# A hybrid decoder block on one core: the branch gates ahead of the branches, 24 of them in pairs by seven block products

## Chip, cores and metric

One core of one Trainium2 chip. The metric is the device time of one execution in microseconds (us).

## What is computed

One layer on 512 tokens of width 2048, in float32: an adaLN-modulated norm, one input projection whose columns go to a gated linear recurrence (HGRN2, 8 heads), to a sliding-window attention and to two sets of branch gates, then a squared-ReLU MLP.

```python
ada = c_act @ w_ada + b_ada                      # six vectors of 2048
h = modulate(rms_norm(x, g1), shift1, scale1)    # (512, 2048)
proj = h @ w_in                                  # hq hf hi hg | aq ak av | gate_hg gate_at
o_hg = rms_norm(hgrn2_chunkwise(...)) * silu(hg)
o_at = sink_swa(q, k, v, sinks, table)
merged = sigmoid(gate_hg) * (o_hg @ w_branch_hg) + sigmoid(gate_at) * (o_at @ w_branch_attn)
x = x + gate1 * (merged @ w_out)
h2 = modulate(rms_norm(x, g2), shift2, scale2)
x = x + gate2 * (square(relu(h2 @ w_ff1)) @ w_ff2)
```

## The kernel before

Everything is held transposed: channels on the 128 partitions, the 512 tokens along the free axis. A product of float32 matrices is made of three matmuls (`mm3`): both operands are split into a high part (a copy by ScalarE) and a low part (a subtraction by VectorE), and high x high, high x low and low x high are added up in PSUM. An output tile of 128 channels over 2048 inputs is 16 x 3 = 48 matmuls of 512 columns.

The work of TensorE is a list of items (`add_tile`, `add_item`); one item is a quarter of such a tile (four input tiles, 12 matmuls) with 512 weight columns. `step` runs item after item: it issues the weight loads on SP (`pump_loads`, three buffers `raw`), the splits of the weights up to two items ahead (`pump_splits`, four buffers `wt`), the item's matmuls, its `post` (what reads PSUM), and one entry of the list `todo`. Everything else, attention, recurrent heads, splits of activations, is a generator that a planner (`Plan`) runs from `drive`, twice in an item: it keeps a clock for each of TensorE, VectorE and ScalarE from fixed costs, and takes a generator's next piece, lowest rank first, when its due time has come and the clocks of VectorE and ScalarE are less than 2.5 us ahead of TensorE's (1 us for rank 9). A piece that yields nothing is due again 0.6 us after the end of its work. The planner decides only the order in which instructions are issued to each engine; the chip then runs each engine's list in that order, with semaphores between them. SBUF slots are counted by tag (`take`, `drop`, `room`: `T` 6, `O` 25, `C` 16, `L` 5).

Stages: a start that makes the first adaLN columns and h; 32 tiles of the input projection for attention and the recurrent heads; then the branches; `wout`; the MLP. In the branch stage (loop at lines 596 to 605) gate tiles and branch tiles alternate: a gate tile (48 matmuls over h) leaves its sigmoid in a slot `T` (`gate_post`), and the branch tile that follows one (first branch) or three (second) gate tiles later (`SKEW`) multiplies its 24 matmuls' result by it (`branch_post`). The last unit of `attention` splits its output at once; that of the recurrent heads is split by `split_hg` after the last tile of the first branch. `ada_rest` (line 397, rank 9) makes the other four adaLN vectors meanwhile: 256 steps, each a load of 256 KB by SP into one of three buffers and a multiply-and-sum by VectorE with a broadcast row `aa` that is loaded once in 16 steps.

```python
while state["item"] < n_start + PACE * n or 0 < len(mg) < KT:
    yield "wait"
```

In the MLP, pairs of output tiles are made with seven block products (Strassen's scheme in Winograd's form) in place of eight: tokens in two halves of 256, inputs and outputs in pairs of tiles (`seven_pair`, line 895). A pair is four units; each is one item of 2 x 7 x 3 matmuls of 256 columns, with seven sums and differences of weight blocks: three are loaded, two more are loaded into a slot `S` to which GpSimd's accumulating DMA adds a fourth block (`pump_loads`), and two are added by VectorE (`split_seven`); a unit takes two of the four `wt` buffers. The input's combinations (`t_sums`, `t_split`) are made once. `sums1` to `sums3` join the seven results, from banks that are four `mx` or one `mx` and three `acc`.

Of the kernel before, what the change touches and what calls it, by code (L numbers as in the profile page):

```python
# [17 lines left out]
P = 128  # L18
# [9 lines left out]
PACE = 1.35  # L28
# [5 lines left out]
SKEW = (1, 3)  # L34
# [57 lines left out]
def tile_block(ctx, tc, xT, cT, wada1, wada2, badaT, g1T, g2T, wg0, win, wbat, wbhg, wout, wfg, wfp, wst,  # L92
               wff2, lbT, hggT, qgT, kgT, sinks, table, ident_d, mask_d, onehot_d, neg_d, outT):
# [243 lines left out]
    def pump_loads():  # L337
        done = items[state["split"]][0] if state["split"] < len(items) else len(loads)
        while state["load"] < len(loads) and state["load"] < done + BUFS["raw"]:
            src, n = loads[state["load"]]  # L340
            if state["load"] in doubled and not room("S") and not room("T", 5):
                return
            raw = act.tile([P, n], F32, tag="raw", bufs=BUFS["raw"], name=nm("raw"))
            if state["load"] in doubled:
                n -= 2 * P
                raw = raw[:, 0:n]
                full, src = src, src[:, 0:n]
            SP.dma_start(out=raw, in_=src)
            if state["load"] in doubled:
                c = 2 * P  # L350
                tag = "S" if room("S") else "T"
# [45 lines left out]
    def ada_rest():  # L397
# [11 lines left out]
        for g in range(4):  # L409
            for q in range(4):  # L410
# [5 lines left out]
                for i in range(16):  # L416
                    fetch(n)
                    while state["item"] < n_start + PACE * n or 0 < len(mg) < KT:
# [6 lines left out]
                    yield  # L425
# [116 lines left out]

    def gate_post(br, n):
        def post(ps):
# [3 lines left out]
            sig[br, n] = t  # L548
        return post

    def branch_post(br, n):
        def post(ps):
# [8 lines left out]
            drop("T")  # L561
            if (br, n) == (0, KT - 1):
# [28 lines left out]
    def gates_done(ps):  # L591
        gate_post(1, KT - 1)(ps)
        drop("A", 32)
        pl.spawn(split_m(), 0)

    for br, wb in ((0, wbat), (1, wbhg)):
        for n in range(KT + SKEW[br]):
            if n < KT:
                add_tile(next_win(), hx, gates_done if (br, n) == (1, KT - 1) else gate_post(br, n))
            if n >= SKEW[br]:  # L600
                def post(ps, br=br, n=n - SKEW[br]):
                    branch_post(br, n)(ps)
                    if br == 1:
                        msdone[n] = True
                add_tile([wb[n - SKEW[br]]], ready(xb[br]), post)

# [39 lines left out]
    HALF = [slice(0, T // 2), slice(T // 2, T)]  # L646
# [3 lines left out]

    def part(xs, c):
        return xs[0][:, c], xs[1][:, c]
# [224 lines left out]
    B22, B11, B12, S1, S3, S2, S4 = range(0, WT, 2 * P)  # L877

    def split_seven(raw, s13, tag):
        hi, lo = wt(), wt()  # L880
        s24 = take("T")
        drop("T")
        c = 2 * P
        sact(hi[:, 0:3 * c], raw[:, 0:3 * c], AF.Copy)
        tt(s24[:, 0:c], s13[:, 0:c], raw[:, c:2 * c], ALU.add)
        tt(s24[:, c:2 * c], s24[:, 0:c], raw[:, 2 * c:3 * c], ALU.add)
        sact(hi[:, 3 * c:5 * c], s13, AF.Copy)
        sact(hi[:, 5 * c:7 * c], s24, AF.Copy)
        tt(lo[:, 0:3 * c], raw[:, 0:3 * c], hi[:, 0:3 * c].bitcast(F32), ALU.subtract)
        tt(lo[:, 3 * c:5 * c], s13, hi[:, 3 * c:5 * c].bitcast(F32), ALU.subtract)  # L890
        tt(lo[:, 5 * c:7 * c], s24, hi[:, 5 * c:7 * c].bitcast(F32), ALU.subtract)
        drop(tag)
        return hi, lo

    def seven_pair(p, now):

        g = p // 2
        cell = {}

        def take_banks():  # L900
            if now:
                cell["b"] = [mx() for _ in range(4)]
            else:
                cell["b"] = [mx()] + [acc() for _ in range(3)]

        def unit(u):
            def emit(hi, lo):
                a, b = HALF
                if u == 0:
                    take_banks()  # L910
                b0, b1, b2, b3 = cell["b"]
                for kp in range(2):
                    j = 2 * u + kp
                    pl.until(lambda: len(tb.get(j, ())) == 4 and isinstance(tb[j][0], tuple))
                    e, o = h2[2 * j], h2[2 * j + 1]
                    t1, t2, t3, t4 = tb[j]
                    first, last = j == 0, j == KT // 2 - 1
                    for ps, c, w, x in ((b0, a, B11, part(e, a)), (b1, a, B12, part(o, a)), (b1, b, S2, t2),
                                        (b2, a, S3, t3), (b2, b, S1, t1), (b3, a, B22, t4), (b3, b, S4, part(o, b))):
                        w += kp * P  # L920
                        mm3(ps[:, c], hi[:, w:w + P], lo[:, w:w + P], x, first and c is a,
                            last and (c is b or ps is b0))
            return emit

        def sums1():
            b0, b1, _, _ = cell["b"]
            e1 = cell["e1"] = take("T", [P, 2, T // 2])
            e2 = cell["e2"] = take("T", [P, 2, T // 2])
            sact(e2[:, 0, :], b0[:, HALF[0]], AF.Copy)
            tt(e1, b1.rearrange("p (n c) -> p n c", n=2), e2[:, 0:1, :].to_broadcast([P, 2, T // 2]), ALU.add)  # L930

        def sums2():
            e1, e2, b2 = cell["e1"], cell["e2"], cell["b"][2].rearrange("p (n c) -> p n c", n=2)
            tt(e2, e1[:, 1:2, :].to_broadcast([P, 2, T // 2]), b2, ALU.subtract)
            tt(e1[:, 1, :], e2[:, 0, :], b2[:, 1, :], ALU.subtract)

        def sums3():
            a, b = HALF
            e1, e2, b3 = cell["e1"], cell["e2"], cell["b"][3].rearrange("p (n c) -> p n c", n=2)
            tt(e2, e2, b3, ALU.add)  # L940
            drop("mx", 4 if now else 1)
# [8 lines left out]
            if now:  # L950
                todo.extend([lambda: hidden(r0, g), lambda: hidden(r1, g)])
# [3 lines left out]
        def post():  # L955
            todo.extend([sums1, sums2, sums3])

        for u in range(4):
            ahead_of[len(items)] = 1 if u < 3 else 2
            ld = add_load(wst[p - 3, u], 1024)  # L960
            doubled.add(ld)
            add_item(ld, 0, 1024, unit(u), None, post if u == 3 else None, split_seven)
# [202 lines left out]
    oat = []  # L1165
# [124 lines left out]
    def attention(c):  # L1290
# [50 lines left out]
        if c == 1:  # L1341
            yield from split_raw(oat, xb[0])
# [175 lines left out]

    ctx.enter_context(tc.manual_schedule())
# [109 lines left out]
```

## Time and profile before

| | |
|---|---|
| median of 3 runs | 2730.06 us (2728.93 to 2730.11) |
| the profiled execution | 2728.55 us, span 2726.8 us |
| TensorE busy | 2698.7 us (99%) |
| TensorE's weight loads | 2289.5 us (84%) |
| VectorE busy | 1683.3 us (62%) |
| ScalarE busy | 1037.1 us (38%) |
| moved by DMA | 415.49 MB, mean 152 GB/s |

PE is TensorE's matmuls and PEld its weight loads, DVE is VectorE, ACT ScalarE, POOL GpSimd and SP the engine whose queue issues most DMAs. L126 and the like are lines of helpers that issue all instructions of a kind (L163 matmuls, L126 sums of two tensors, L159 ScalarE's operations), so groups are told apart by their tiles. Busy shares are averages over stages.

### The profile page before, as it was taken

Reading aid. Unit: us, or ns where it says so; the run is one execution under the profiler, and the core shown is the slowest. Engines: PE = TensorE matmul, PEld = TensorE weight load, DVE = VectorE, ACT = ScalarE, POOL = GpSimd, SP = SyncE. Lnnn points to the kernel's source line nnn. Section 1 sums busy time; section 2 is a strip of 40 time slices with the busy share of each in tenths; the row PEclk is TensorE's granted clock in tenths of the full one; section 3 lists DMA queues with packets and bytes.
Section 4 is the critical chain, followed back from the end, with each engine's and each line's share of the span. In section 5 each row is a group of like instructions: output and inputs, shape, how many; then the busy total and the mean of one; then the engine's idle time right before and its main releaser. Section 6 shows DMA issues by size and latency. Waiting matters only on the chain.

```text
span 2726.8 us, 38611 instructions
## 1 busy us (share of the span) xinstructions
PE 2698.7 (99%) x14718; PEld 2289.5 (84%) x14718; DVE 1683.3 (62%) x3231; ACT 1037.1 (38%) x1913; POOL 153.3 (6%) x144
## 2 busy tenths in 40 slices
PE   8999999999999999999999999999999999999999
PEld 4777777888888888888888899988999988999887
DVE  5778787655444545565467666666566655666664
ACT  4245455544222322232353434333343333434332
POOL 1000000000000000000000101110011100111100
PEclk9999999999999999999999999999999999999999
DMA  8852322344555555556334455654455544555544
GB/s 329 293 182 97 128 89 74 127 137 147 192 182 184 195 187 179 192 168 211 108 93 123 130 134 138 156 141 127 129 144 147 148 129 126 138 147 148 137 126 132
DMA packets 182073, 415.49 MB, mean 152 GB/s; under 512 B 18880, under 2 KB 48704, under 8 KB 181888
## 3 DMA queue, kind: packets, MB, share of 16 engines
q1 hardware_dynamic: 149184, 380.18, 42.4%
q0 software_dynamic: 32704, 32.85, 7.8%
q8 instruction: 116, 1.90, 0.3%
q14 instruction: 69, 0.57, 0.1%
HBM read 408.72 MB, written 4.23 MB: 151 GB/s over the span
## 4 chain that ended last, share of the span: by engine, by line
PE 95%; DVE 3%; ACT 1%; DMA 1%; issue 0%; SPq 0%; POOLq 0%; ACTq 0%
PE acc L163 69%; PE mx L163 25%; PE mx L167 1%; DVE wt L126 1%; DVE T L126 0%; DMA C<-xT 0%; DMA S<-wst 0%; ACT T L159 0%; DVE C L130 0%; DVE L L130 0%; ACT wt L159 0%; DVE B L130 0%; ACT A L159 0%; DVE T L130 0%; DVE s L1242 0%
## 5 line engine op out<-in xcount | busy, mean ns | idle before, releaser
L163 PE MATMUL acc<-A,wt 128*128 128x512 f32 (+1 forms) x5136 | 1134.1, 369 | 4.1 <-ACT A L159 1.9
L163 PEld LDWEIGHTS acc<-A,wt 128*128 128x128 f32 x5136 | 908.7, 189 | 174.9 <-issue 8.6
L126 DVE TENSOR_TENSOR wt<-raw,wt 128x512 fp32r<-128x512 f32 (+1 forms) x828 | 595.8, 724 | 422.7 <-ACT wt L159 419.6
L159 ACT ACTIVATE wt<-raw 128x512 fp32r<-128x512 f32 (+1 forms) x828 | 529.9, 657 | 841.1 <-PE acc L163 592.5
L163 PE MATMUL acc<-B,wt 128*128 128x512 f32 (+1 forms) x3528 | 732.6, 359 | 2.6 <-DVE wt L126 1.2
L163 PEld LDWEIGHTS acc<-B,wt 128*128 128x128 f32 x3528 | 610.1, 189 | 101.8 <-DVE wt L126 1.8
L163 PE MATMUL mx<-A,wt 128*128 128x256 f32 (+1 forms) x2448 | 426.1, 310 | 5.4 <-DVE wt L126 3.0
L163 PEld LDWEIGHTS mx<-A,wt 128*128 128x128 f32 x2448 | 360.6, 192 | 37.0 <-issue 5.0
L163 PE MATMUL mx<-B,wt 128*128 128x256 f32 (+1 forms) x1632 | 297.5, 319 | 0.4 <-DVE wt L126 0.4
L130 DVE SCALAR_TENSOR_TENSOR C<-acc,adaT,C 128x512 f32<-128x512 f32 x210 | 157.3, 749 | 199.5 <-PE acc L163 199.5
L163 PEld LDWEIGHTS mx<-B,wt 128*128 128x128 f32 x1632 | 249.7, 191 | 21.6 <-DVE wt L126 0.9
L354 POOL DMA_DIRECT2D S<-wst x88 | 105.2, 1196 | 2123.0 <-DVE T L126 1203.1
L421 DVE SCALAR_TENSOR_TENSOR ada<-ada,aa 128x512 f32<-128x512 f32 x256 | 175.3, 685 | 45.8 <-DMA ada<-wada 41.2
L163 PE MATMUL acc<-O,wt 128*128 128x512 f32 x768 | 178.6, 389 | 0.0
L163 PEld LDWEIGHTS acc<-O,wt 128*128 128x128 f32 x768 | 144.2, 188 | 29.9
L159 ACT ACTIVATE T<-T 128x256 f32<-128x256 f32 (+1 forms) x218 | 104.4, 507 | 110.2 <-DVE T L126 107.7
L159 ACT ACTIVATE wt<-T 128x512 fp32r<-128x512 f32 x144 | 87.2, 621 | 83.9 <-DVE T L126 79.0
L126 DVE TENSOR_TENSOR wt<-T,wt 128x512 fp32r<-128x512 f32 x144 | 96.2, 684 | 0.0
L126 DVE TENSOR_TENSOR T<-T,raw 128x256 f32<-128x256 f32 x144 | 61.1, 425 | 32.9 <-DMA T<-wst 29.0
L159 ACT ACTIVATE T<-acc 128x512 f32<-128x512 f32 x34 | 20.3, 598 | 160.2 <-PE acc L163 160.2
L159 ACT ACTIVATE B<-T 128x512 fp32r<-128x512 f32 x80 | 47.2, 602 | 47.4 <-DVE T L126 33.1
L126 DVE TENSOR_TENSOR T<-S,raw 128x256 f32<-128x256 f32 x88 | 37.1, 421 | 41.6 <-DMA S<-wst 37.1
(170 smaller groups left out, 1349.9 us busy)
## 6 DMA issues: line engine op xcount, KB each, us to landing
raw<-win SPq DMA_DIRECT2D x128, 512.0 KB, 4.0
ada<-wada SPq DMA_DIRECT2D x256, 256.0 KB, 4.3
raw<-wff SPq DMA_DIRECT2D x128, 512.0 KB, 3.6
raw<-wst SPq DMA_DIRECT2D x116, 384.0 KB, 3.8
O<-wada SPq DMA_DIRECT2D x128, 256.0 KB, 5.1
S<-wst SPq DMA_DIRECT2D x88, 256.0 KB, 3.7
S<-wst POOLq DMA_DIRECT2D x88, 256.0 KB, 4.3
raw<-wout SPq DMA_DIRECT2D x32, 512.0 KB, 4.0
```

Of the source, the lines that this page charges most:

```text
L126: nc.vector.tensor_tensor(out=out, in0=in0, in1=in1, op=op)
L130: nc.vector.scalar_tensor_tensor(out=out, in0=in0, scalar=scalar, in1=in1, op0=op0, op1=op1)
L159: nc.scalar.activation(out=out, in_=in_, func=func, **kw)
L163: PE.matmul(out, lhsT=lhsT, rhs=rhs, start=start, stop=stop)
L167: PE.transpose(out=out, in_=in_, identity=ident)
L354: G.dma_start(out=s.rearrange("p (n c) -> p n c", c=c), in_=full[:, None, 3 * c:4 * c].to_broadcast([P, 2, c]), accum_op=ALU.add)
L421: nc.vector.scalar_tensor_tensor(out=t, in0=t, scalar=1.0, in1=cb, op0=ALU.mult, op1=ALU.mult, accum_out=adaq[:, i, q:q + 1])
```

## The change

The 32 gate tiles come before both branches: first the 16 of attention (branch 0), then the 16 of the recurrent heads (branch 1). The first 8 stay plain tiles; the other 24 are made in 12 pairs by seven block products, with the MLP's code, which moves up into `add_seven` and gets one more call of the planner in a unit. The combinations of h that these need are made by a new generator, `h_blocks` (rank 5), once attention is over, in slots `O` (9), `L` (3) and `C` (15, after the last recurrent head); the last of the four overwrites half of a tile of h. The weight tensor of the 24 tiles is laid out in blocks on the host's side like that of the MLP. The doubled weight loads use slots `L` before the MLP. Sigmoids are written to DRAM by SP (`spill`, taken from `todo` in a later place) and read back ahead of each branch tile, up to three at a time (`sig_load`). Attention's output is split after the last gate pair. The number of items that weights are split ahead is worked out from the `wt` buffers that they hold. `ada_rest` is paced by one step an item, no longer pauses while `merged` is split, and yields `go`, which makes it due again at once.

```diff
-PACE = 1.35
+PACE = 1.0
-SKEW = (1, 3)
+NCG = 8
...
+            slot = "S" if "mlp" in pools else "L"
-            if state["load"] in doubled and not room("S") and not room("T", 5):
+            if state["load"] in doubled and not room(slot) and not room("T", 5):
...
-                    while state["item"] < n_start + PACE * n or 0 < len(mg) < KT:
+                    while state["item"] < n_start + PACE * n:
                         yield "wait"
...
-                    yield
+                    yield "go"
...
             t = take("T")
             sact(t, ps, AF.Sigmoid)
-            sig[br, n] = t
+
+            def spill():
+                SP.dma_start(out=sigd[br, n], in_=t)
+                drop("T")
+            todo.append(spill)
...
+    def sig_load(k):
+        def pre():
+            for i in range(k, min(k + 3, 2 * KT)):
+                if i not in fetched and (i == k or room("T", 2)):
+                    fetched.add(i)
+                    t = sig[i // KT, i % KT] = take("T")
+                    SP.dma_start(out=t, in_=sigd[i // KT, i % KT])
+        return pre
...
+    def h_blocks():
+        a, b = HALF
+        while len(att_done) < 2:
+            yield "wait"
+        homes = ["O"] * 9 + ["L"] * 3 + ["C"] * 15
+        for j in range(KT // 2):
+            own = j < 3
+            tags = [homes.pop(0) for _ in range(4 if own else 3)]
+            while "C" in tags and len(ohg) < NH:
+                yield "wait"
...
+            yield from need("T", 4)
+            e, o = full(h[2 * j]), full(h[2 * j + 1])
+            x, y = take("T"), take("T")
+            tt(x[:, a], e[:, b], e[:, a], ALU.subtract)
+            tt(x[:, b], x[:, a], o[:, b], ALU.subtract)
+            tt(y[:, a], e[:, b], o[:, b], ALU.subtract)
+            tt(y[:, b], o[:, b], o[:, a], ALU.subtract)
+            tt(y[:, b], y[:, b], x[:, a], ALU.subtract)
...
+            split(y, hi, lo)
+            t2 = two(tags[2])
+            split(x[:, b], *t2)
...
+        for j in range(3, KT // 2):
+            while state["item"] < last_plain + j // 2 + 2:
+                yield "wait"
+            e = full(h[2 * j])
+            tt(e[:, a], e[:, b], e[:, a], ALU.subtract)
+            hb[j][0] = part(h[2 * j], b)
+            split(e[:, a], *hb[j][0])
...
+        def post():
+            todo.extend([sums1, sums2, sums3])
+            if done:
+                done()
...
+            sact(e1[:, 0, :], e1[:, 0, :], AF.Sigmoid)
+            sact(e2[:, 0, :], e2[:, 0, :], AF.Sigmoid, scale=-1.0)
+            sact(e1[:, 1, :], e1[:, 1, :], AF.Sigmoid, scale=-1.0)
+            sact(e2[:, 1, :], e2[:, 1, :], AF.Sigmoid)
...
+    def gates_done():
         drop("A", 32)
-        pl.spawn(split_m(), 0)
+        drop("O", 9)
+        drop("L", 3)
+        drop("C", 15)
+        pl.spawn(split_raw(oat, xb[0]), 0)
+        pl.spawn(split_m(), 1)
...
+    for k in range(NCG):
+        last_plain = len(items)
+        add_tile(next_win(), hx, gate_post(k // KT, k % KT))
+    for k in range(NCG, 2 * KT, 2):
+        add_seven([wgt[(k - NCG) // 2, u] for u in range(4)], gate_blocks, k % 4 == 0, gate_joined(k),
+                  gates_done if k == 2 * KT - 2 else None)
...
     for br, wb in ((0, wbat), (1, wbhg)):
-        for n in range(KT + SKEW[br]):
...
+        for n in range(KT):
+            add_tile([wb[n]], ready(xb[br]), branch_post(br, n), sig_load(KT * br + n))
...
+    held_by = [2 if e[6] is split_seven else 1 for e in items]
+    for i in range(len(items)):
+        n = AHEAD
+        while sum(held_by[i:i + n + 1]) > BUFS["wt"]:
+            n -= 1
+        ahead_of.setdefault(i, n)
...
+    pl.spawn(h_blocks(), 5)
     pl.spawn(ada_rest(), 9)
     while state["item"] < len(items):
-        if state["item"] == n_mix:
-            pl.until(lambda: len(oat) == 8)
+        if state["item"] == n_mix + 4 * NCG:
+            pl.until(lambda: len(att_done) == 2)
         step()
```

## Rows read from the trace of the kernel before

**Rows 1.** The page: engine table (busy, share, instructions), and chain that ended last.
```profile
PE 2698.7 (99%) x14718; PEld 2289.5 (84%) x14718; DVE 1683.3 (62%) x3231; ACT 1037.1 (38%) x1913; POOL 153.3 (6%) x144
...
PE 95%; DVE 3%; ACT 1%; DMA 1%; issue 0%; SPq 0%; POOLq 0%; ACTq 0%
```

**Rows 2.** Waits of PE, whole span: us in total, times, longest us.
```profile
PE mx L163 <- DVE wt L126: 3.4, 5, 1.2
...
PE mx L167 <- DVE T L126: 0.9, 2, 0.4
```

**Rows 3.** Timeline of PE, 590 to 706 us: start, length, operation, count.
```profile
592.79 0.33 PE L163 MATMUL mx<-T,C 128*128 128x64 f32 x2
...
643.98 0.33 PE L163 MATMUL mx<-T,C 128*128 128x64 f32 x2
...
684.27 5.60 PE L163 MATMUL acc<-O,wt 128*128 128x512 f32 x24
689.71 11.04 PE L163 MATMUL acc<-A,wt 128*128 128x512 f32 x48
700.59 5.60 PE L163 MATMUL acc<-O,wt 128*128 128x512 f32 x24
```

**Rows 4.** Timeline of PE in a pair of the MLP.
```profile
2007.23 0.52 PE L163 MATMUL acc<-A,wt 128*128 128x256 f32 x3
2007.59 0.52 PE L163 MATMUL mx<-A,wt 128*128 128x256 f32 x3
```

**Rows 5.** Windows: stretch, length, busy us of PE, PEld, DVE, ACT, POOL; PEclk, DMA share, GB/s.
```profile
20.00:60.00 40.00, 36.60 (x166) 22.79 (x161) 22.24 (x46) 15.19 (x27) 0.51 (x1) 0.96 0.91 348
480.00:560.00 80.00, 79.55 (x412) 64.44 (x410) 50.61 (x107) 39.00 (x68) 0.00 (x0) 1.00 0.42 138
560.00:640.00 80.00, 80.00 (x393) 65.28 (x390) 46.31 (x99) 43.55 (x78) 0.00 (x0) 1.00 0.39 125
760.00:960.00 200.00, 200.00 (x884) 165.69 (x883) 100.88 (x225) 55.73 (x95) 0.00 (x0) 1.00 0.57 188
1994.00:2014.00 20.00, 20.00 (x169) 20.00 (x168) 14.39 (x25) 8.21 (x15) 4.79 (x4) 1.00 0.78 187
```

**Rows 6.** Timeline of DVE in a pair of the MLP; brackets: idle before, releaser.
```profile
1999.03 0.42 DVE L126 TENSOR_TENSOR T<-S,raw 128x256 f32<-128x256 f32 x1 [0.88 <-DMA S<-wst]
1999.49 0.43 DVE L126 TENSOR_TENSOR T<-T,raw 128x256 f32<-128x256 f32 x1
...
2006.08 0.96 DVE L126 TENSOR_TENSOR wt<-raw,wt 128x768 fp32r<-128x768 f32 x1 [1.75 <-ACT wt L159]
2006.95 0.68 DVE L126 TENSOR_TENSOR wt<-S,wt 128x512 fp32r<-128x512 f32 x1
2007.55 0.68 DVE L126 TENSOR_TENSOR wt<-T,wt 128x512 fp32r<-128x512 f32 x1
```

**Rows 7.** The page: DMA issues, count, KB each, median us to landing.
```profile
S<-wst SPq DMA_DIRECT2D x88, 256.0 KB, 3.7
S<-wst POOLq DMA_DIRECT2D x88, 256.0 KB, 4.3
```

**Rows 8.** Timeline of DVE, 640 to 940 us.
```profile
648.52 0.69 DVE L421 SCALAR_TENSOR_TENSOR ada<-ada,aa 128x512 f32<-128x512 f32 x1 [1.86 <-DMA ada<-wada]
...
674.90 0.75 DVE L130 SCALAR_TENSOR_TENSOR O<-mx,hgg_sb,C 128x512 f32<-128x512 f32 x1
...
935.86 0.69 DVE L126 TENSOR_TENSOR O<-O,O 128x512 fp32r<-128x512 f32 x1 [4.62 <-ACT O L159]
936.47 0.68 DVE L126 TENSOR_TENSOR wt<-raw,wt 128x512 fp32r<-128x512 f32 x1
```

**Rows 9.** Windows of line 421 alone (steps of ada, two instructions each).
```profile
200.00:480.00 280.00, 17.29 (x50) 1.00 0.28 95
```

**Rows 10.** Tile ada, 480 to 660 us: who waited for it; landing.
```profile
  DVE ada L421: 9.1, 6
...
DMA to landing us min/median/max: 4.0/4.5/5.2
```

More of the change, by code (lines that the diff above doesn't have):

```diff
@@ L541, in tile_block @@
     mg = []
+    sigd = {(br, n): dram.tile([P, T], F32, name=f"sig{br}_{n}") for br in range(2) for n in range(KT)}
     def gate_post(br, n):
@@ new lines, in tile_block, with part, full, two @@
+    hb = {}
+    hbdone = set()
+    att_done = []
+    def part(xs, c):
+        return xs[0][:, c], xs[1][:, c]
+    def full(xs):
+        t = take("T")
+        tt(t, xs[0].bitcast(F32), xs[1].bitcast(F32), ALU.add)
+        return t
+    def two(tag):
+        z = take(tag, [P, 2, T // 2], F32R)
+        return z[:, 0, :], z[:, 1, :]
+    def h_blocks():
[8 more added lines that the diff above has]
+                yield "wait"
+            for tag in set(tags):
+                yield from need(tag, tags.count(tag))
+            yield from need("T", 4)
[6 more added lines that the diff above has]
+            tt(y[:, b], y[:, b], x[:, a], ALU.subtract)
+            drop("T", 2)
+            yield
+            hi, lo = take(tags[0], dt=F32R), take(tags[1], dt=F32R)
+            split(y, hi, lo)
+            t2 = two(tags[2])
+            split(x[:, b], *t2)
+            t1 = None
+            if own:
+                t1 = two(tags[3])
+                split(x[:, a], *t1)
+            drop("T", 2)
+            hb[j] = [t1, t2, (hi[:, a], lo[:, a]), (hi[:, b], lo[:, b])]
+            if own:
+                hbdone.add(j)
+            yield
+        for j in range(3, KT // 2):
+            while state["item"] < last_plain + j // 2 + 2:
+                yield "wait"
+            yield from need("T")
+            e = full(h[2 * j])
+            tt(e[:, a], e[:, b], e[:, a], ALU.subtract)
+            hb[j][0] = part(h[2 * j], b)
+            split(e[:, a], *hb[j][0])
+            drop("T")
+            hbdone.add(j)
+            yield
@@ L875, in ff2_post @@
         return post
[L877 to L893, printed above, removed]
@@ L895, in seven_pair @@
-    def seven_pair(p, now):
[L897 to L937, printed above, removed]
@@ L938, in sums3, with hidden_blocks, joined @@
+    def hidden_blocks(j):
+        a, b = HALF
+        pl.until(lambda: len(tb.get(j, ())) == 4 and isinstance(tb[j][0], tuple))
+        e, o = h2[2 * j], h2[2 * j + 1]
+        return [part(e, a), part(o, a), part(o, b)] + tb[j]
+    def seven_pair(p, now):
+        def joined(e1, e2):
             a, b = HALF
[L939 to L941 removed]
             r0, r1 = take("T"), take("T")
@@ L950, in sums3 @@
             if now:
-                todo.extend([lambda: hidden(r0, g), lambda: hidden(r1, g)])
+                todo.extend([lambda: hidden(r0, p // 2), lambda: hidden(r1, p // 2)])
             else:
                 waiting.extend([r0, r1])
[L955 to L962, printed above, removed]
+        add_seven([wst[p - 3, u] for u in range(4)], hidden_blocks, now, joined)
     def ff2_group(g):
@@ L1340, in attention @@
         drop("O", 4 + 6)
-        if c == 1:
-            yield from split_raw(oat, xb[0])
+        att_done.append(c)
     ohg = []
@@ L1579 @@
              .reshape(8, G0 // 4, P, 1024))
-    win = kxn(w_in[:, sum(tiles[G0:], [])])
+    win = kxn(w_in[:, sum(tiles[G0:NCG - 2 * KT], [])])
+    wgt = sevens(w_in[:, sum(tiles[NCG - 2 * KT:], [])])
     rows = []
```

114 lines of the change are left out of this document (93 added, 21 removed).

## The prediction

> **What bounds the kernel now.** I read the page's engine table and chain first: TensorE is busy 99% of the span and nearly all of the chain that ended last is its matmuls [rows 1]. The list of what TensorE waited for then shows how little it stands: its largest wait on weight splits is 3.4 us in the whole span [rows 2]. So a change pays by the matmul columns that it removes, and loses by each microsecond in which it makes TensorE wait. The profiled execution took 2728.55 us (span 2726.8), 1.5 us under the median of 2730.06; I work against it and add the 1.5 at the end.
>
> **The products saved.** A gate tile is 48 matmuls of 512 columns. In the gate stage one tile takes 700.59 - 689.71 = 10.88 us, 226.7 ns for each [rows 3], so two tiles take 21.76 us. A pair by seven products is 8 x 7 x 3 = 168 matmuls of 256 columns. The MLP already does this: a block of three follows the next at 0.36 us, 120 ns each [rows 4], and not 113.3, since the weight loads there fill the whole window, 20.00 of 20.00 us [rows 5]. A pair is 20.16 us, 1.60 less. Twelve pairs: -19.2 us. The other eight gates and all branch tiles keep their matmuls. The Trainium skill, TensorE: Matmul & The Clock Gate, section Back-to-back issue gap, has N/2.4 + 2.5 ns for a matmul; by it two tiles would take 20.7 us, a pair 18.3, and the saving would be 28 us as an estimate. The rows stand against it at both widths, 226.7 and 120 ns, so it gets no chance as a rival, and the sum keeps the rows.
>
> All that follows is what the change pays for it. The granted clock is 1.00 in every stage concerned [rows 5], and no stall below is long, so I cost nothing for it.
>
> **VectorE's split work in the pairs.** A unit (four to a pair, 5.04 us of TensorE) costs VectorE two sums at 0.46, a split of 768 at 0.87 and two of 512 at 0.60: 3.0 us [rows 6]. The joins of a pair are three operations of 512 and one of 256, 2.3 us, so 0.6 for each unit, and one step of the ada matrix, of the same shape as the splits of 512, is 0.6. Together 4.2 of 5.04 us, 83%, against 50% in the gate stage of before [rows 5]. It fits on average. The MLP runs the same units with 72% of VectorE [rows 5] and TensorE doesn't wait there. The order is the risk: a unit's split can start only when the unit before last has returned its weight buffers, so it has 5.04 us, and the join, which waits for the pair's last products, stands ahead of it on VectorE.
>
> **The doubled loads.** Each unit needs a load (3.7 us) and behind it the accumulating load of GpSimd (4.3) [rows 7], with only two slots (in `L`, as three of its five now hold blocks of h) and a third in `T` once in a pair. The third unit's slot is returned 2.4 us into a unit, and its data are wanted 7.7 us later, while the two loads need 8 and their issues 0.6: about 1 us late. The MLP lives with this lateness: VectorE waits for S there 0.88 us [rows 6], and it is hidden. New is the company: ada steps (256 KB a unit) and spills (128 KB a unit). In the MLP's units the DMA engines are 0.78 busy at 187 GB/s; the gate stage needs 0.57 for 188 GB/s [rows 5]. At that price ada's 52 GB/s adds 0.16, and spills of 26 GB/s some 0.08 to 0.10: 1.02 to 1.04. In the startup 0.91 of busy carried 348 GB/s [rows 5], so a busy engine moves more bytes than these shares say, and I take 265 GB/s to be carried with loads 1 to 2 us later than now. The third unit's split then ends at most about 0.5 us after TensorE wants it. Bounds: 0 (hidden as in the MLP) to 1.2 us a pair, 0 to 14 us; I take 0.2 a pair, 2 us.
>
> **Blocks of h.** `h_blocks` needs for each of 8 pairs of h tiles about 4.3 us of VectorE (two sums of 512, five of 256, splits of 512 and 256), and later 5 times 1.5. Three pairs can be made once attention is over; five need the slots of the last recurrent head, whose last operation is at 674.90 [rows 8]. The gate stage begins near 659 (684.27 less two tiles and 3.6 us of that head [rows 3]); eight plain tiles last 87 us, so the first seven-product unit starts near 750. Between 675 and 750 TensorE runs 27 items, and VectorE has 2.1 us free in each: 57 us for these 21.5 and 7.5 and for ada's 27 steps (16). No wait; bounds 0 to 4, taken 0.5.
>
> **The spills.** SP waits for the sigmoid of each plain gate before it issues the write, behind which stand the next weight load and ada loads. A plain item's weights are split up to three items (8 us) early, and the write is held about 3.3 us: hidden at one ada step an item; 0 to 6 us, taken 1. In the pairs the spill comes one step after the sigmoids and holds nothing.
>
> **The pace of ada.** The step of VectorE that builds the late adaLN columns is asked for once an item (was 1.35), its pause is dropped, and it yields `go`: the planner may put several in a row, as long as its clock for VectorE is under 1 us ahead. Before, at most one went in at a time. By 480 us only 25 steps had run (each shows two instructions) [rows 9]; heads come every 51.2 us [rows 3] with 16 items, so 480 us is item 120 and the new rule wants 72. Some 40 are owed when VectorE gets free. The planner doesn't know what a load costs: three buffers and 4.5 us to landing [rows 10] give three steps in about 5 us, 1.67 us a step, where the plan counts 0.68. VectorE executes in order, so a step whose load is late holds the splits and the recurrence behind it. This is seen already: 1.86 us at 648.52 [rows 8], 9.1 us in six waits over the stage [rows 10], of which TensorE felt little: it waited for such a result twice, 0.4 us at most [rows 2]. With two steps an item, the loads need 3.3 us where an item with its share of the head lasts 3.2. So I expect small delays in bursts of 16 steps (then a pause of two items for the next `aa`), about 1 us in each of five bursts. Bounds 0 to 18; taken 4, and 0.5 more for attention (0 to 4). The steps themselves hide in idle time of VectorE, 58 to 63% busy here [rows 5].
>
> **The two joints.** Before, gate tiles stood between the branches: `split_hg` ran from 935.86 [rows 8] under gates of the second branch. Now branch 1 follows branch 0 at once. VectorE must first multiply the last tile (0.6, after TensorE's end), then make the first low half (0.6): TensorE stands 1.1 us or more, and longer where an ada step comes between two splits, as at 936.47 and after. 1 to 5, taken 2. The start of branch 0 is milder, as the splits of `oat` wait only for the first join, whose banks are finished some 1.4 us before the unit ends: 0 to 4, taken 1. The sigmoid loads are issued up to two tiles ahead, so nothing.
>
> After the branches, gates' absence and ada's earlier end free VectorE in `wout`, where TensorE didn't wait: nothing. The MLP's units keep their code; one split there now stands behind the join: 0.
>
> **Sum.** -19.2 + 2 + 0.5 + 1 + 4 + 0.5 + 2 + 1 = -8.2 us: 2720.3 against 2728.55, and 2722 as a median.
>
> **Rivals.** (1) All of it is hidden. For: TensorE's waits of before are tiny although VectorE often waited for loads. Only the joint of 1.1 us and some start cost remain, -17.5: 2712. (2) The pairs become bound by the loads. For: shares that add up above 1, and a slot chain that is already 1 us late. The Trainium skill, DMA: Bandwidth & Descriptors, section Issuing engines are not separate DMA queues, says that transfers of all issuers share the same engines; the trace agrees as far as GpSimd's and SP's loads together give the 0.78 [rows 5]. Against: those 0.91 at 348 GB/s. With 1.2 us a pair the sum is +4: about 2734. (3) Slower: the bursts of ada hold VectorE. The place is 480 to 750 us, where 40 owed steps, the three early blocks and the recurrence meet. If the planner really places two and a half steps an item, the loads need 4.2 us for each 3.2 us item: 1 us an item over 30 to 40 items, less what the early splits cover, 25 us in place of 4. It decides once more than about two steps an item are placed for ten items on end. Against: the gap at each new `aa`, and idle time of VectorE that takes some of it. 2743. (4) The seven-product matmuls don't reach 120 ns; nothing speaks for it, the MLP's blocks are the same.
>
> **How the numbers follow.** The likeliest has 0.45 (2715 to 2726), rival 1 0.14, rival 2 0.20, rival 3 0.17, the rest 0.04. The range 2711 to 2738 takes in rivals 1 and 2 and the likeliest, and leaves out most of rival 3 (its 0.17 and a little). About 0.2% (5.5 us) is what a measurement can tell from no change. Under 2724.6 lie rival 1 and nearly all of the likeliest: 0.58. Within, 0.25: most of rival 2 and an end of the likeliest. Above 2735.5: 0.17.
>
> **What would show it.** The pair stage should have 168 matmuls in 20.2 us and 12 pairs in 242 us, where before 24 tiles took 261. If right, the waits of TensorE on weight splits stay under 5 us in that stage, and a single wait of 1 to 3 us stands where branch 1 begins. If rival 2, VectorE's waits for S or T loads grow past 2 us each and TensorE waits for `wt` once in each pair. If rival 3, waits of VectorE on ada loads grow from 9 us to over 40 between 480 and 750, and TensorE waits there for VectorE. I'd be wrong altogether if TensorE's total at the stages outside the pairs changed with no wait beside it.

## The result, and the profile after

The changed kernel takes 2833.28 us (median; 2827.75 to 2836.45) against 2730.09 for the kernel before: a ratio of 1.0376, with a 95% interval of 1.0358 to 1.0394. It is 103 us slower, where 8 us faster was forecast. Its profiled execution took 2832.76 us with a span of 2830.9.

The page of after, engine table and chain that ended last, as in [rows 1]:

```profile
PE 2726.9 (96%) x15582; PEld 2343.7 (83%) x15582; DVE 1827.7 (65%) x3513; ACT 1092.3 (39%) x2019; POOL 210.7 (7%) x192
...
PE 74%; DMA 12%; DVE 9%; issue 3%; ACT 2%; SPq 0%; POOL 0%; DVEq 0%; POOLq 0%; ACTq 0%
PE acc L163 51%; PE mx L163 23%; DMA L<-wgt 5%; DMA ada<-wada 4%; DVE wt L126 4%; DVE T L126 2%; DVE ada L422 1%; DMA S<-wst 1%; PE mx L167 1%; DMA T<-wgt 1%; ACT T L159 1%; ACT wt L159 0%; DMA T<-wst 0%; DVE C L126 0%; DVE C L130 0%
```

TensorE's matmuls fell from 95% of the chain to 74%. In their place stand loads (12% in place of 1%), mainly the doubled loads of the pairs' weights (`L<-wgt`) and the ada matrix (`ada<-wada`), and VectorE's work (9% in place of 3%).

Windows by stage, columns as in [rows 5]: first gates and branches of before in one, then of after the plain gates, the pairs, the branches, and the output projection with the start of the MLP.

```profile
658.70:1184.70 526.00, 526.00 (x2334) 434.93 (x2333) 270.78 (x598) 147.07 (x255) 0.00 (x0) 1.00 0.55 182
```

```profile
660.60:767.60 107.00, 97.38 (x417) 77.56 (x415) 75.34 (x189) 31.98 (x63) 2.44 (x2) 0.95 0.71 220
767.60:1072.60 305.00, 266.27 (x2014) 261.62 (x2014) 198.13 (x382) 115.98 (x206) 54.96 (x46) 0.92 0.78 202
1072.60:1284.30 211.70, 188.87 (x769) 149.90 (x769) 141.31 (x301) 55.66 (x98) 0.00 (x0) 0.93 0.65 216
1284.30:1460.00 175.70, 175.70 (x822) 147.48 (x820) 66.34 (x102) 50.27 (x86) 0.00 (x0) 1.00 0.37 120
```

At the rates of before (226.7 and 120 ns a matmul) the three stages need 90.6 (384 matmuls and 3.6 us of a head), 241.9 and 174.1 us: 506.6, which is 526.0 less the 19.3 saved. They take 623.7. Of the 117 us too much, TensorE stood idle for 71 (length less busy: 9.6, 38.7, 22.8) and was busy 46 us longer than its matmuls need (6.8, 24.4, 14.8). That second part is the clock: before it was granted at 1.00 throughout, now at 0.95, 0.92 and 0.93, and the missing 0.05, 0.08 and 0.07 of the three lengths are 5.4, 24.4 and 14.8 us.

What PE waited for in the whole span (us, times, longest), as in [rows 2]:

```profile
PE mx L163 <- DVE wt L126: 41.5, 23, 5.4
PE acc L163 <- DVE wt L126: 22.1, 18, 3.1
PE acc L163 <- DVE O L126: 10.2, 7, 2.6
```

What DVE waited for, first in the pairs (760 to 1090 us), then from 480 to 760:

```profile
DVE T L126 <- DMA L<-wgt: 75.4, 30, 6.8
DVE ada L422 <- DMA ada<-wada: 21.9, 13, 3.6
...
DVE ada L422 <- DMA ada<-wada: 51.5, 28, 4.0
```

Up to 660 us alone the ada waits are 26.6 us, where before had 9.1 [rows 10]. The ada steps alone, two instructions each, as in [rows 9]:

```profile
200.00:480.00 280.00, 24.30 (x72) 1.00 0.34 109
480.00:660.00 180.00, 39.94 (x118) 1.00 0.54 170
660.00:760.00 100.00, 27.69 (x81) 0.96 0.69 216
760.00:1060.00 300.00, 29.78 (x90) 0.91 0.78 203
1060.00:1260.00 200.00, 52.12 (x152) 0.92 0.69 229
```

One place in the plain gates shows a whole loss, on DVE and on PE (timeline; in brackets the idle time before, and what ended it):

```profile
727.04 0.69 DVE L422 SCALAR_TENSOR_TENSOR ada<-ada,aa 128x512 f32<-128x512 f32 x1 [3.81 <-DMA ada<-wada]
727.66 0.08 DVE L422 DVE_READ_ACCUMULATOR ada<-ada,aa 128x1 f32 x1
727.66 0.69 DVE L126 TENSOR_TENSOR wt<-raw,wt 128x512 fp32r<-128x512 f32 x1
```

```profile
728.40 7.33 PE L163 MATMUL acc<-A,wt 128*128 128x512 f32 x24 [1.86 <-DVE wt L126]
```

VectorE stands 3.81 us for an ada load with the split behind it, and TensorE waits 1.86 us for that split. The 24 matmuls that follow need 5.4 us and take 7.3, at a granted clock of 0.77 where the 11.7 us before the wait had 1.00: the clock costs as much again as the wait.

### The profile page after: what moved, and what is told of

Same layout as the page of the kernel before. It is cut to its first block, busy times and chain, and to the rows that moved or that the text cites. A ratio compares the mean times of both kernels' runs of the same rounds, so it can differ in the third digit from the quotient of the medians.

```text
span 2830.9 us, 41201 instructions
## 1 busy us (share of the span) xinstructions
PE 2726.9 (96%) x15582; PEld 2343.7 (83%) x15582; DVE 1827.7 (65%) x3513; ACT 1092.3 (39%) x2019; POOL 210.7 (7%) x192
## 4 chain that ended last, share of the span: by engine, by line
PE 74%; DMA 12%; DVE 9%; issue 3%; ACT 2%; SPq 0%; POOL 0%; DVEq 0%; POOLq 0%; ACTq 0%
PE acc L163 51%; PE mx L163 23%; DMA L<-wgt 5%; DMA ada<-wada 4%; DVE wt L126 4%; DVE T L126 2%; DVE ada L422 1%; DMA S<-wst 1%; PE mx L167 1%; DMA T<-wgt 1%; ACT T L159 1%; ACT wt L159 0%; DMA T<-wst 0%; DVE C L126 0%; DVE C L130 0%
## 5 line engine op out<-in xcount | busy, mean ns | idle before, releaser
L163 PE MATMUL acc<-A,wt 128*128 128x512 f32 (+1 forms) x4362 | 942.9, 358 | 12.1 <-DVE wt L126 9.4
L163 PEld LDWEIGHTS acc<-A,wt 128*128 128x128 f32 x4362 | 752.6, 191 | 141.4 <-DVE wt L126 12.8
L163 PE MATMUL mx<-A,wt 128*128 128x256 f32 (+1 forms) x3114 | 536.1, 307 | 45.4 <-DVE wt L126 40.0
L163 PEld LDWEIGHTS mx<-A,wt 128*128 128x128 f32 x3114 | 455.5, 194 | 80.9 <-DVE wt L126 43.4
L163 PE MATMUL acc<-O,wt 128*128 128x512 f32 (+1 forms) x936 | 218.3, 389 | 22.8 <-DVE wt L126 10.7
L163 PEld LDWEIGHTS acc<-O,wt 128*128 128x128 f32 x936 | 176.1, 200 | 61.9 <-DVE O L126 14.7
L159 ACT ACTIVATE wt<-T 128x512 fp32r<-128x512 f32 x204 | 125.9, 625 | 139.8 <-DVE T L126 99.4
L126 DVE TENSOR_TENSOR wt<-T,wt 128x512 fp32r<-128x512 f32 x204 | 136.1, 683 | 0.0
L126 DVE TENSOR_TENSOR T<-T,raw 128x256 f32<-128x256 f32 x204 | 86.7, 425 | 53.9 <-DMA T<-wst 45.4
L355 POOL DMA_DIRECT2D L<-wgt x36 | 43.1, 1197 | 609.1 <-DMA L<-wgt 461.1
```

The costliest lines, as they stand in the source:

```text
L126: nc.vector.tensor_tensor(out=out, in0=in0, in1=in1, op=op)
L159: nc.scalar.activation(out=out, in_=in_, func=func, **kw)
L163: PE.matmul(out, lhsT=lhsT, rhs=rhs, start=start, stop=stop)
L355: G.dma_start(out=s.rearrange("p (n c) -> p n c", c=c), in_=full[:, None, 3 * c:4 * c].to_broadcast([P, 2, c]), accum_op=ALU.add)
```

## Experiments

Two suspects stand in these rows. **Theory A**: the ada steps, by how many of them come close together. **Theory B**: the two loads behind each other that a unit of the pairs needs, too slow whatever ada does; **theory C** is its later form, that GpSimd's accumulating loads run one at a time. Theories D and E are two forms of A: the rate of the steps, or the amount of their loads. Single executions are given as one figure; the kernel before took 2730.9 to 2731.3 beside them.

### One part at a time

**All 32 gates plain**: order, sigmoids in DRAM and ada as changed, no pairs.

```diff
-NCG = 8
+NCG = 32
...
-    for k in range(NCG, 2 * KT, 2):
-        add_seven([wgt[(k - NCG) // 2, u] for u in range(4)], gate_blocks, k % 4 == 0, gate_joined(k),
-                  gates_done if k == 2 * KT - 2 else None)
...
-    pl.spawn(h_blocks(), 5)
```

> The changed kernel with all 32 gates as plain tiles: no pairs and no blocks of h, but gates ahead of the branches, sigmoids by way of DRAM, and ada as changed. Matmuls as in the kernel before. Theory A: the plain gates and the branches lose as in the changed kernel, 16 us in 8 tiles and 38 us in 32 branch tiles, so 2770 to 2800. Theory B: only the two joints cost, 2732 to 2742.

Measured: 2773.47 us, 42.5 over before. From 700 to 800 us TensorE is busy 82%, at a clock of 0.91; from 800 to 1000 it stands nowhere, and from 1000 to 1200 for 3 us, not the 38 that were expected in the branches. So a large loss needs no pair.

**Before, with ada's rules alone** (the pace, the pause, the `go`).

```diff
-PACE = 1.35
+PACE = 1.0
...
-                    while state["item"] < n_start + PACE * n or 0 < len(mg) < KT:
+                    while state["item"] < n_start + PACE * n:
...
-                    yield
+                    yield "go"
```

> The kernel before with the three changes to ada alone: pace 1.0, no pause, `go`. Theory A: waits on ada loads of over 50 us while the steps owed are caught up, and TensorE stalls of 10 to 40 us: 2740 to 2770. Theory B: within 5 us of the kernel before.

Measured: 2752.8 us, 22 over before. Windows of it, columns as above:

```profile
660.00:700.00 40.00, 39.51 (x187) 31.58 (x186) 25.05 (x68) 13.88 (x29) 0.00 (x0) 1.00 0.72 225
700.00:760.00 60.00, 48.02 (x179) 36.58 (x178) 34.09 (x91) 10.59 (x18) 0.00 (x0) 0.89 0.70 214
760.00:860.00 100.00, 100.00 (x443) 82.78 (x442) 52.33 (x124) 25.65 (x43) 0.00 (x0) 1.00 0.62 209
```

The loss is where owed steps are caught up: some 18 of the 22 us in 660 to 760 us, with 55 steps, and most of the rest from 480 us on. Later 101 steps in 300 us cost nothing: it isn't ada's bytes but its rate.

**After without ada** (its steps and loads left out, so the late adaLN vectors are not computed).

```diff
-    pl.spawn(ada_rest(), 9)
```

> The changed kernel without the 256 steps and loads of ada after the start; the late adaLN vectors are left at their bias, all else is computed. Theory A: all stages come near their matmuls, 2712 to 2722. Theory B: the pairs still take 280 us or more and VectorE still waits over 50 us for the doubled loads there, while plain gates and branches are free of waits: 2750 to 2775.

Measured: 2757.05 us. 76 of the 103 us go with ada; the pairs still take 282 us. GpSimd's issues of accumulating loads in that kernel, and the DVE operations that need them:

```profile
860.27 1.20 POOL L355 DMA_DIRECT2D L<-wgt  x1 [5.60 <-DVE wt L126]
868.87 1.19 POOL L355 DMA_DIRECT2D T<-wgt  x1 [7.40 <-issue]
873.73 1.20 POOL L355 DMA_DIRECT2D L<-wgt  x1 [3.67 <-issue]
```

```profile
868.57 0.42 DVE L126 TENSOR_TENSOR T<-L,raw 128x256 f32<-128x256 f32 x1 [6.35 <-DMA L<-wgt]
873.44 0.89 DVE L126 TENSOR_TENSOR T<-T,raw 128x256 f32<-128x256 f32 x2 [0.86 <-DMA T<-wgt]
```

```profile
866.90:870.50 3.60, 1.35 (x12) 1.15 (x11) 1.90 (x4) 1.64 (x3) 1.19 (x1) 1.00 0.00 0
```

The second issue is 0.30 us after the operation that had waited for the first load, the third 0.29 us after the next. Of 29 such waits in the pairs, 19 are followed by the next issue at 0.29 or 0.30 us, and none earlier. So these loads run one behind the other, each some 4.2 to 4.9 us in quiet and 6.5 to 8.3 where the loads of two units and four spills are issued just ahead; and from 866.90 to 870.50 the DMA engines move nothing at all (share 0.00), though the next load is due. The Trainium skill, DMA: Bandwidth & Descriptors, section Anatomy of one DMA, puts about 2 us of a GpSimd transfer down to setup and completion together, most of it to the completion. Here 1.67 us of the gap lie before the operation that waited for the load (868.57) and 1.93 behind it, of which 0.30 are up to the next issue. A unit of TensorE lasts 5.04 us, 48 of them in a row: little is left to make up a slow one. What makes GpSimd wait is not named ("issue").

**The accumulating loads**: without ada (left out again), once with a third slot in `L` and no fallback to `T`, once without such loads in the gate pairs: all 512 KB of a unit come in one load, and GpSimd adds the two blocks in SBUF.

```diff
-        homes = ["O"] * 9 + ["L"] * 3 + ["C"] * 15
+        homes = ["O"] * 9 + ["L"] * 2 + ["C"] * 16
...
-            if state["load"] in doubled and not room(slot) and not room("T", 5):
+            if state["load"] in doubled and not room(slot) and (slot == "L" or not room("T", 5)):
```

> Without ada (as the run before that left it out; late adaLN vectors stay at their bias). Three slots L in place of two for the doubled loads of the pairs, by moving one block of h from L to C, and none of these loads into T, so that never two units' loads are issued together. Theory C, formed from the trace without ada: GpSimd's accumulating loads run one at a time (the next starts 0.3 us after the one before has landed), 4.5 us each when the queues are quiet and over 8 when two units' loads and four spills are issued ahead of it. C says pairs of 242 to 255 us and no accumulating load over 6.5 us: 2716 to 2730. If instead the DMA engines are simply full in this stage, the pairs stay at 275 to 285 and the total at 2750 to 2758.

```diff
...
+                if slot == "S":
...
+                else:
+                    for i in range(2):
+                        G.tensor_tensor(out=s[:, i * c:i * c + c], in0=raw[:, i * c:i * c + c], in1=raw[:, 3 * c:4 * c],
+                                        op=ALU.add)
...
```

> Without ada (late adaLN vectors at their bias). In the gate pairs the whole 512 KB of a unit is loaded once and GpSimd adds the two weight blocks itself in SBUF, so there is no second load and no accumulating load there (512 KB a unit in place of 896). The MLP's pairs are left. Theory C: pairs of 241 to 248 us, 2712 to 2720. If GpSimd's adding slows VectorE or takes over 4 us a unit, pairs over 255 and total over 2728.

Measured: 2722.8 and 2720.87 us, pairs of 250 and 244 us. Windows of the pairs, without ada (282 us), then with GpSimd's additions:

```profile
749.40:1031.50 282.10, 259.98 (x2018) 256.99 (x2016) 169.64 (x294) 116.25 (x206) 53.78 (x45) 0.94 0.72 174
```

```profile
748.40:993.00 244.60, 243.06 (x2018) 242.16 (x2016) 211.84 (x296) 111.06 (x206) 97.24 (x90) 1.00 0.41 129
```

The accumulating loads cost 36 us without ada. The same matmuls now run at a clock of 1.00, and near the 241.9 us that 120 ns give. Both kernels lie 8 to 10 us under before, but without ada.

With three slots the bytes are the same (DMA share 0.79) and the loads still run one behind the other, some of them for 6.6 to 8.1 us against the 6.5 that were expected at most; yet 34 of the 36 us are back. So it is not the DMA engines' capacity: one behind the other was too late with two slots and `T`, and a third slot in place of `T` gives the lead that hides it.

GpSimd's additions are not free for VectorE. Its 512-column splits take 0.68 us, and 1.23 beside an addition (rows of VectorE, then of GpSimd); its operations in the pairs, 294 and 296 by the windows, take 211.8 us in place of 169.6. Without ada TensorE feels next to nothing of it.

```profile
864.19 0.68 DVE L126 TENSOR_TENSOR wt<-L,wt 128x512 fp32r<-128x512 f32 x1
...
868.74 1.23 DVE L126 TENSOR_TENSOR wt<-L,wt 128x512 fp32r<-128x512 f32 x1
```

```profile
867.89 2.67 POOL L361 TENSOR_TENSOR T<-raw 128x256 f32<-128x256 f32 x2 [0.94 <-DMA raw<-wgt]
```

### How ada is placed

**One step a drive until the output projection, then `go`.**

```diff
-                    yield "go"
+                    yield "go" if state["item"] >= n_out else None
```

> The changed kernel, but a step of ada yields nothing in place of `go` until wout begins, so at most one goes in at a call of the planner, as in the kernel before; the pace of one an item and all else stay. Theory A (the bursts of ada, whose loads the plan doesn't count, hold VectorE and crowd the DMA engines): the waits on ada loads between 480 and 1260 us fall from 94 us to under 30, plain gates and branch tiles lose most of their 16 and 38 us, and the pairs most of their 63: 2730 to 2755. Theory B (the two loads behind each other, with two slots and one in T, are too slow for a unit of 5.04 us whatever ada does): the pairs stay above 290 us where 242 would do, the branches improve: 2775 to 2805.

Measured: 2851.05 us, worse by 18. In the pairs little is gained (302 us); 80 steps are left for the output projection and burst there (TensorE busy 80% from 1300 to 1400). The burst moved with its loss.

**Steps due 1.57 us apart, with credit for two**, in after, and with GpSimd's additions:

```diff
-                    e[2] = now + 1.0 if r == "wait" else 0.0 if r == "go" else self.last + 600.0
+                    e[2] = now + 1.0 if r == "wait" else max(e[2], now - 3000.0) + 1570.0 if r == "go" else self.last + 600.0
```

> The changed kernel, but the planner counts what ada's loads cost: after a step the next is due 1.57 us of its clock later, with credit for two loads already made, in place of at once. Number of steps, pace and all else as changed. If the bursts are what ada costs: waits on ada loads under 40 us in the whole span (100 as changed), plain gates within 95 us and branches within 185 (107 and 212 as changed), pairs near the 282 us that they took without ada: 2760 to 2775. If it is the amount of ada's traffic: pairs stay over 300 us and the total over 2785.

> The two together with all of ada and so the whole result: GpSimd adds the blocks in the gate pairs, and ada's steps come due by their loads. If bursts of ada and accumulating loads are the whole cause, what is left over the matmuls is small: pairs under 250, branches under 183, plain gates under 95: 2715 to 2728, faster than both kernels. If ada costs by its amount, 2735 to 2760.

Measured: 2826.37, and 2776.63 us (ratio 1.0167, interval 1.0137 to 1.0197). Both theories missed the second. Pacing by the time of a load is not enough: 0.6 steps a us are still allowed, 47 of them stand in 1060 to 1160, and TensorE waits up to 5.9 us for the splits with which a branch starts.

**Steps spaced 2.6 us, no tie to items, and none while a branch's inputs are split**; with GpSimd's additions, and in after:

```diff
-                    e[2] = now + 1.0 if r == "wait" else 0.0 if r == "go" else self.last + 600.0
+                    e[2] = now + 1.0 if r == "wait" else max(e[2], now - 2600.0) + 2600.0 if r == "go" else self.last + 600.0
...
-                    while state["item"] < n_start + PACE * n:
+                    while joint[0] and len(xb[0]) < 8 or joint[1] and len(xb[1]) < 8:
                         yield "wait"
...
+                joint[1] = True
...
+        joint[0] = True
```

> After, with the blocks of the gate pairs added by GpSimd in SBUF (as in e7_pool_add), all ada steps kept, and ada under another rule: a step may follow the one before it after 2.6 us of the planner's clock, never two at once, no tie to the item count, and none while the outputs that a branch waits for are split. By the planner's own order the last steps come in the output projection. Theory D (ada costs only where its steps come faster than its loads, or between the splits at a joint; the loads as such are free): 2720.87 of e7_pool_add plus a few us, 2721 to 2732. Theory E (the 64 MB of ada's loads cost wherever they lie once the pairs need their own): at least half of the 56 us between e8_pool_due and e7_pool_add stays, 2748 to 2777.

> After, with ada's new rule of e9_spaced alone; the accumulating loads of the pairs stay. Theory D with theory C (GpSimd's accumulating loads cost some 35 to 40 us whatever ada does): 2757.05 of e2_noada plus a few us, 2755 to 2772. If ada's loads also lengthen the accumulating loads: 2780 to 2800. If the pairs' loads cost only together with ada's bursts: below 2745.

Measured: 2743.69 (ratio 1.0054, interval 1.0037 to 1.0071) and 2794.46 us (1.0235, 1.0220 to 1.0250). Of the 56 us that ada cost in the kernel with GpSimd's additions 23 are left: less than the half that E asks for, more than D's few. Where and how close the steps stand was most of ada's cost; spacing and hold changed together here, and the hold is taken out alone below. The second shows that the causes feed each other: with ada spaced, the accumulating loads cost 51 us (36 without ada), the pairs take 303. A part of the rest of the first is a burst at the end, where the planner must have all steps; PE in the output projection:

```profile
1360.68 5.60 PE L163 MATMUL acc<-A,wt 128*128 128x256 f32 x34 [11.94 <-DVE wt L126]
```

**Spacing 2.3 us**, so that the last step comes earlier, with GpSimd's additions, and with three slots in their place:

```diff
-                    e[2] = now + 1.0 if r == "wait" else max(e[2], now - 2600.0) + 2600.0 if r == "go" else self.last + 600.0
+                    e[2] = now + 1.0 if r == "wait" else max(e[2], now - 2300.0) + 2300.0 if r == "go" else self.last + 600.0
```

> e9_spaced with one size changed: 2.3 us of the planner's clock between ada steps in place of 2.6. In e9_spaced 13 steps are left when the output projection must have them all, and they run in one burst: VectorE 1347.73 to 1359.94, TensorE waits 11.94 us and works at half clock behind it. With 2.3 us the planner's order has the last step 9 items earlier. Theory D (rate, not amount): the wait and its clock cost go, 2743.69 less 15 to 19, so 2724 to 2729, below the 2729.53 of before by 0 to 0.2%. Theory E (the amount of loads costs): the rate of the branch stage rises and its waits come back, 2738 or more.

> After with ada's rule of e11_spaced23 and the three slots of e6_slots (one h block moved from L to C, no fallback to T); the accumulating loads stay. Without ada e6_slots took 2722.8. If ada's loads lengthen the accumulating loads whatever runs ahead of them: 2745 to 2780. If three slots give enough spare: 2725 to 2735.

Measured: 2735.69 (1.0018, 1.0009 to 1.0027) and 2753.51 us (1.0080, 1.0066 to 1.0094). The wait of 11.94 us is gone, but 8 us came back, not 15 to 19: the pairs grew from 250.4 to 257.3 us, with 40 steps in them both times. Both theories missed the figure. Three slots, enough without ada, are not enough beside its loads (pairs 272 us).

**What is left**: thinner steps in the pairs (9.0 us apart there, 2.0 elsewhere), and 2.3 us without the hold at the branches.

```diff
+def gap():
+    return 9000.0 if pairs[0] else 2000.0
...
+                    e[2] = now + 1.0 if r == "wait" else max(e[2], now - gap()) + gap() if r == "go" else self.last + 600.0
...
+        pairs[0] = items[i][6] is split_seven and "mlp" not in pools
...
```

```diff
-                    while joint[0] and len(xb[0]) < 8 or joint[1] and len(xb[1]) < 8:
-                        yield "wait"
```

> e11_spaced23 with ada's spacing changed by stage: 9.0 us of the planner's clock between steps in the gate pairs, 2.0 elsewhere. By the planner's order 23 steps in place of 40 stand in the pairs, and the last one still comes before the end of the output projection. In e11_spaced23 the pairs take 257.3 us, in e7_pool_add (no ada) 244.4, and VectorE is busy 117 of 125 us there. If that fullness is what is left of the cost: pairs near 250, 2735.69 less 4 to 8, 2728 to 2732. If what is left is the loads themselves: no change in the pairs, or the denser steps elsewhere take it back, 2735 to 2745.

> e11_spaced23 without the hold: ada steps may stand between the splits that the start of each branch waits for. If the steps at the joints cost anything once they are spaced: 2 to 6 us more, 2738 to 2742, with waits of TensorE on O above e11's 2.4 us in the span. If only bursts did harm there: within 1 us of 2735.69.

Measured: 2729.51 us (ratio 0.9999, 0.9989 to 1.0008), pairs 250.4; and 2748.28 us (1.0065, 1.0051 to 1.0079). With 23 steps in place of 40 the pairs give back their 7 us. That VectorE, busy 238 of 257 us there, was what was left is not shown: fewer steps are fewer loads too, and with steps 2.6 us apart the pairs took the same 250.4 us with 40 of them and VectorE busy 233. And the hold is worth 12.6 us, more than expected: PE where branch 0 begins, without the hold, then with it (both 2.3 us apart):

```profile
1011.08 0.96 PE L163 MATMUL acc<-O,wt 128*128 128x512 f32 x3 [2.54 <-DVE O L126]
1014.34 4.51 PE L163 MATMUL acc<-O,wt 128*128 128x512 f32 x9 [2.29 <-DVE O L126]
1019.63 0.97 PE L163 MATMUL acc<-O,wt 128*128 128x512 f32 x3 [0.78 <-DVE O L126]
1023.37 16.92 PE L163 MATMUL acc<-O,wt 128*128 128x512 f32 x61 [2.78 <-DVE O L126]
```

```profile
1011.03 2.34 PE L163 MATMUL acc<-O,wt 128*128 128x512 f32 x9 [0.30 <-DVE O L126]
1013.89 0.97 PE L163 MATMUL acc<-O,wt 128*128 128x512 f32 x3 [0.52 <-DVE O L126]
```

Nine matmuls take 4.51 us behind the second wait (granted clock 0.50) and 2.34 in the other kernel (1.00); behind the first wait the three still ran at 1.00 (0.96 us). The version with all its work and thin steps ends level with before: the 19.3 us that the products save are spent again. Some 9 of them go with ada, by the last link of the chain below; about as much is spent without ada too, 2.5 us of it in the pairs, and the runs do not divide the rest.

The chain of the runs: 2833.3, ada spaced and held 2794.5 (-38.8), GpSimd's additions 2743.7 (-50.8), no burst at the end 2735.7 (-8.0), thin in the pairs 2729.5 (-6.2), no ada at all 2720.9 (-8.6).

## Why the prediction was wrong, point by point

- **The products saved: right.** The pairs reach 120 ns a matmul where nothing waits (244 us for twelve pairs, 241.9 worked out), and the rows of the MLP [rows 4] held. Rival 4 is out.
- **Clock at no cost: wrong, and it runs through every term.** "No stall below is long, so I cost nothing for it" is the step that failed. Behind waits such as the 1.86 us one at 728.40 the granted clock fell, and 46 of the 117 us are busy time too long. I had the bounds in waits only; 71 us of waits became 117, some 1.65 for each.
- **The doubled loads: mechanism named (rival 2), size wrong.** Taken 2 us, bound 14; measured 36 alone and 51 beside ada. Its sign came: VectorE's waits for `L` are 2.5 us on average and up to 6.8, and TensorE waited for `wt` 16 times in the twelve pairs. The step that failed compared shares of the DMA engines (1.02 to 1.04 against 0.91 at 348 GB/s) and concluded that loads come 1 to 2 us later. The DMA share of that stage is 0.78, far from full. What the runs showed in its place is that accumulating loads follow one another, each 4.2 to 8.3 us without ada against 5.04 of a unit, with two slots and `T` too little lead; a third slot hid all but 2 us without ada, and not beside its loads. The MLP's hidden wait of 0.88 us [rows 6] was no proof: it is one of 35, the longest 4.4 us (row below, VectorE in before), and the MLP has eight units on end and then 46 us without such an issue (2008.03 to 2055.66), where the gates have 48 units on end, with ada and spills beside them.

```profile
DVE T L126 <- DMA S<-wst: 37.1, 35, 4.4
```

- **The pace of ada: mechanism named (rival 3), place and size wrong.** Taken 4, bound 18, rival 25 us between 480 and 750. Up to the end of the plain gates after loses 18 us (1.9 before they begin, 16 in them), so there the rival was near, and its sign came (46.1 us of ada waits from 480 to 750, over 40 asked); but ada costs 76 us in all of after, and 22 on the kernel before. The step that failed looked at one place only: steps are still owed in the branches, since the pairs take only 45 steps in 300 us for their 48 items, and 76 follow in 1060 to 1260. The count of items, on which the new pace rests, slows in the pairs: one has four items of 5.04 us where two plain gates have eight. I worked out the owed steps at 480 us and not at 1060.
- **The joints: too small.** 3 us taken, 9 at most. Branch 0 alone shows waits of 1.93, 1.46, 1.90, 2.64 and 1.27 us (PE, 1074 to 1090), and even with spaced steps 12.6 us come back when none stands between the splits. The prediction saw the steps "as at 936.47 and after" [rows 8], but not that each of them can wait for its own load there, though in before the one at 943.84 did (1.24 us).
- **Blocks of h: small, as forecast, but not nothing.** The first unit with seven products starts at 766 in after, 749 without ada. Two waits of TensorE, 2.9 us together, are for the late half tiles in `A`, inside the bound of 4; taken were 0.5.

```profile
792.17 0.96 PE L163 MATMUL mx<-A,wt 128*128 128x256 f32 x3 [2.33 <-ACT A L159]
```

- **Spills in the plain gates: not separated.** Nothing was run that takes them away alone; without ada the plain gates lose nothing (89 us for 89 busy), so at most ada with them.
- **VectorE's split work: fits, as forecast.** VectorE is busy 198 of the 305 us of the pairs (65%, 83 worked out). Only GpSimd's additions, which the prediction doesn't have, bring it to 92%.
- **Adding the terms.** All were costed one by one beside the old neighbours. Loads, ada and waits share VectorE's order: with both causes in place 103 us, with ada gone 27, with the loads and ada's placement cured 0. The rivals were kept apart, each with the others at their small values, so the range left out the case in which two come together.

## What to carry to other kernels

A wait that TensorE feels can cost twice, once as a wait and once as matmuls at the lower clock behind it; here 46 us of that came to 71 us of waits, so price both. Background work that needs a load for each step is to be spaced in time over all stages, and kept off the moments when another engine waits for the same queue; a pace in items changes when the items change length. Before a chain of accumulating loads is taken over from another stage, compare its longest link, not its mean, with the time of a unit, and ask what rests the old place had. When work is moved to an engine that stands idle, look at what its neighbours' operations then take.

## What the runs showed of the hardware

- Accumulating loads of GpSimd: the next was never issued earlier than 0.29 us after the one before had been waited for and landed, and the DMA engines can stand at 0.00 meanwhile (866.90 to 870.50 us without ada). Plain additions by GpSimd in SBUF (two for each unit) cost TensorE next to nothing without ada, pairs of 244 us with GpSimd busy 97, but they lengthen VectorE's operations beside them: 1.23 us in place of 0.68 for a 512-column split (868.74 and 864.19), 42 us in all over the twelve pairs.
- The clock: three matmuls of 512 columns take 0.96 us at a granted clock of 1.00 and 1.65 at one of 0.50 (rows at 1011.08, and 1081.10 below), and 24 take 7.33 in place of 5.4 at 0.77 (728.40). The Trainium skill, TensorE: Matmul & The Clock Gate, Part 1, has two levels only, 1.2 and 2.4 GHz; the rows agree: behind a wait of 2.72 us at 1055.93, 256-column matmuls start 0.21 us apart in place of 0.12, at a granted clock of 0.50 (1057.50 to 1058.50).

```profile
1057.52 0.41 PE L163 MATMUL acc<-O,wt 128*128 128x256 f32 x1
1057.73 0.41 PE L163 MATMUL acc<-L,wt 128*128 128x256 f32 x1
1057.94 0.41 PE L163 MATMUL acc<-O,wt 128*128 128x256 f32 x1
...
1081.10 1.65 PE L163 MATMUL acc<-O,wt 128*128 128x512 f32 x3 [1.90 <-DVE O L126]
```
